# Gathers that convert fp32 rows to fp16 in flight, drains by tile, and a variable lead, in a gather, cumulative sum and matmul kernel

## The chip, the cores and the metric

The kernel runs on one core of one Trainium2 chip. The metric is the time on the device in microseconds (us), as the median over several executions. A ratio between two kernels is the mean time of one kernel's fast runs over the mean of the other's fast runs of the same rounds, so it is not quite the ratio of the medians quoted beside it.

The chips that these runs fell on are of two kinds. On two of them (numbers 1 and 6), and in the recorded result, the kernel before takes 351 us. On five others (2, 7, 10, 13 and 15) the same kernel takes longer. I call these **quick chips** and **slow chips**. Whether it is the chip itself or its condition at the time isn't shown: numbers 10 and 13 were slow in both of their calls, and every other chip was seen in one call only. Within one call the runs of the kernel before lie within 0.7% of each other on a quick chip and within 1 to 3.5% on a slow one. Every call runs the kernel before on the same chip as its experiments.

## The reference

```python
B, S, N, D = (16, 4096, 2048, 512)            # x: fp32 [B, S, D], indices: int64 [B, N], sorted, w: fp32 [D, D]

def reference(x, indices, w):
    gathered = x[np.arange(B)[:, None], indices, :]
    cs = np.cumsum(gathered, axis=1)
    return np.matmul(cs, w).astype(np.float32)
```

The kernel gathers 16 x 2048 rows of 2 KB, 67.1 MB, and writes as many bytes of output. A tile is 128 rows; there are T = 256 tiles, and a pair of tiles is a group g (R = 2, G = 128).

## The kernel before

Each tile goes through seven steps on five engines: GpSimd issues the gather, ScalarE casts the rows to fp16, TensorE sums them with a triangular matrix ("sums"; the result is transposed and lies in PSUM, the memory for TensorE's results), VectorE adds the running total and writes fp16 ("carry"), TensorE multiplies by w ("project"; the result is a "product"), ScalarE copies the product out of PSUM ("drain"), and SyncE starts the store. `Lane.need(sem, value)` waits on a semaphore unless that engine has already waited for as much.

```python
    def gather(t):                                   # GpSimd
        g, r = divmod(t, R)
        if g >= NG // R:                             # NG = 16 tiles of fp32
            pool.need(s_c0, R)
            pool.need(s_c, g - NG // R)              # its buffer is free when its cast is done
        ...
        nc.gpsimd.indirect_dma_start(out=g32[g % (NG // R)][:, r, :], in_=x_flat, ...).then_inc(s_g[t % NG], 16)

    def cast(g):                                     # ScalarE, a pair at a time
        for t in range(R * g, R * g + R):
            act.need(s_g[t % NG], 16 * (t // NG + 1))
        act.need(s_a, R * (g - NH + 1))
        nc.scalar.copy(out=g16[g % NH][:], in_=g32[g % (NG // R)][:]).then_inc(s_c, 1)

    def sums(t, first=0):                            # TensorE: 4 matmuls of 128 columns, after s_c
    def carry(t):                                    # VectorE: adds the last column of the tile before
    def project(g, j, first=0):                      # TensorE: 4 matmuls of 512 columns
    def drain(g):                                    # ScalarE: a pair out of PSUM
    ...
    for g in range(G - 1):                           # the order on ScalarE
        if g + AH + 1 < G - 1:                       # AH = 2
            cast(g + AH + 1)
        ...
        drain(g)
```

ScalarE executes in order, so drain(g) stands behind cast(g + 3).

Of the kernel before, what the change touches and what calls it, by code (L numbers as in the profile page):

```python
# [27 lines left out]
def kernel(  # L28
# [21 lines left out]
    NH = 4  # L50
    NA = 4
    NB = 2
    NC = 4
    NO = 8
    LOOP = 4
    AH = 2
# [13 lines left out]
    ut = const.tile([P, R, Q], FP16)  # L70
    ident = const.tile([P, P], FP32)
    zeros = const.tile([P, D], FP16)
    spare = const.tile([P, 1], FP16)
    g32 = [const.tile([P, R, D], FP32, name=f"g32_{i}") for i in range(NG // R)]
    g16 = [const.tile([P, R, D], FP16, name=f"g16_{i}") for i in range(NH)]
# [3 lines left out]
    pb = [ps.tile([P, R, D], FP32, name=f"pb{i}") for i in range(NB)]  # L79
# [3 lines left out]
    def sem(name):  # L83
        return tc.alloc_semaphore(name)

    s_z, s_ut, s_wc, s_if, s_pt, s_prep, s_c0, s_c1 = (
        sem(f"s_{n}") for n in ("z", "ut", "wc", "if", "pt", "prep", "c0", "c1")
# [8 lines left out]
    s_c = sem("s_c")  # L96
# [9 lines left out]
    def gather(t):  # L106
        g, r = divmod(t, R)
        if g >= NG // R:
            pool.need(s_c0, R)
            pool.need(s_c, g - NG // R)  # L110
# [3 lines left out]
        else:  # L114
# [3 lines left out]
            out=g32[g % (NG // R)][:, r, :],  # L118
# [6 lines left out]
    def cast(g):  # L125
        for t in range(R * g, R * g + R):
            act.need(s_g[t % NG], 16 * (t // NG + 1))
        act.need(s_a, R * (g - NH + 1))
        nc.scalar.copy(out=g16[g % NH][:], in_=g32[g % (NG // R)][:]).then_inc(s_c, 1)  # L129

    def cast_tile(t, done):
        g, r = divmod(t, R)
        act.need(s_g[t % NG], 16 * (t // NG + 1))
        act.need(s_a, R * (g - NH + 1))
        nc.scalar.copy(out=g16[g % NH][:, r], in_=g32[g % (NG // R)][:, r]).then_inc(done, 1)  # L135

    def sums(t, first=0):
        g, r = divmod(t, R)
        if isinstance(first, int):
            if g in (0, G - 1):  # L140
                pe.need(s_c1 if g else s_c0, r + 1)
            else:
                pe.need(s_c, g)
            pe.need(s_ut, 4)
            pe.need(s_d, t - NA + 1)
        elif r == 0:
            nc.tensor.wait_ge(s_c, first + g)
        for c in range(DC):
            mm = nc.tensor.matmul(  # L149
                out=pa[t % NA][:, c],  # L150
                lhsT=g16[g % NH][:, r, c * P : (c + 1) * P],
                rhs=ut[:],
                start=(c == 0),
                stop=(c == DC - 1),
            )
        mm.then_inc(s_a, 1)

    def carry(t):
        g, r = divmod(t, R)
        dve.need(s_b, R * (g - NC + 1))  # L160
        dve.need(s_a, t + 1)
        dst = cst[g % NC][:, :, :, r * Q : (r + 1) * Q]
        if t % NT == 0:
            nc.vector.tensor_copy(out=dst, in_=pa[t % NA][:]).then_inc(s_d, 1)  # L164
            return
        e = (r - 1) % R
        last = cst[(t - 1) // R % NC][:, :, R - 1, e * Q + Q - 1 : e * Q + Q]
        dve.need(s_d, t)
        nc.vector.tensor_tensor(  # L169
            out=dst,  # L170
            in0=pa[t % NA][:],
            in1=last.unsqueeze(2).broadcast_to([P, DC, R, Q]),
            op=mybir.AluOpType.add,
        ).then_inc(s_d, 1)

    def project(g, j, first=0):
        if isinstance(first, int):
            pe.need(s_wc, DC)
            pe.need(s_d, R * (g + 1))
            pe.need(s_e, g - NB + 1)  # L180
        elif j == 0:
            nc.tensor.wait_ge(s_d, R * first + R * (g + 1))
            nc.tensor.wait_ge(s_e, first + (g - NB + 1))
        for c in range(DC):
            mm = nc.tensor.matmul(  # L185
                out=pb[g % NB][:, j],
                lhsT=cst[g % NC][:, c, j, :],
                rhs=w16[:, c, :],
                start=(c == 0),
                stop=(c == DC - 1),  # L190
            )
        mm.then_inc(s_b, 1)

    def drain(g):
        act.need(s_o[g % NO], 16 * (g // NO))
        act.need(s_b, R * (g + 1))
        nc.scalar.copy(out=ob[g % NO][:], in_=pb[g % NB][:]).then_inc(s_e, 1)  # L197

    def store(g):
        b, h = divmod(g, GB)  # L200
        dst = out[b, h * R * P : (h + 1) * R * P, :].rearrange("(p j) d -> p j d", j=R)
        sp.need(s_e, g + 1)
        nc.sync.dma_start(out=dst, in_=ob[g % NO][:]).then_inc(s_o[g % NO], 16)

    def drain_last(j, lane, copy):
        g = G - 1
        lane.need(s_o[g % NO], 16 * (g // NO))
        lane.need(s_b, R * g + j + 1)
        copy(out=ob[g % NO][:, j], in_=pb[g % NB][:, j]).then_inc(s_el[j], 1)  # L209

    def store_last():
        b, h = divmod(G - 1, GB)
        dst = out[b, h * R * P : (h + 1) * R * P, :].rearrange("(p j) d -> p j d", j=R)
        for j in range(R):
            sp.need(s_el[j], 1)
            nc.sync.dma_start(out=dst[:, j], in_=ob[(G - 1) % NO][:, j]).then_inc(s_ol[j], 16)
# [11 lines left out]
    idx_rows = indices.bitcast(U32).rearrange("b (t q) -> (b t) q", q=2 * P)  # L228
    for k in range(KI):
# [3 lines left out]
    for c in range(DC):  # L233
# [144 lines left out]
```

## Time and profile before

| | |
|---|---|
| time, median (recorded result, 4 runs) | 351.19 us (350.31 to 352.29) |
| span of its trace | 451.1 us |
| work that the time must hold | 67.1 MB gathered, 67.1 MB stored, w and the indices: 135.66 MB |

The trace lies 100 us above the timed runs (the prediction had three of these, median 351.63 us). The lines of its trace are shown and read in the prediction below.

### The profile page before, as it was taken

Reading aid. Unit: us, or ns where it says so; the run is one execution under the profiler, and the core shown is the slowest. Engines: PE = TensorE matmul, PEld = TensorE weight load, DVE = VectorE, ACT = ScalarE, POOL = GpSimd, SP = SyncE. Lnnn points to the kernel's source line nnn. Section 1 sums busy time; section 2 is a strip of 40 time slices with the busy share of each in tenths; the row PEclk is TensorE's granted clock in tenths of the full one; section 3 lists DMA queues with packets and bytes.
Section 4 is the critical chain, followed back from the end, with each engine's and each line's share of the span. In section 5 each row is a group of like instructions: output and inputs, shape, how many; then the busy total and the mean of one; then the engine's idle time right before and its main releaser. Section 6 shows DMA issues by size and latency. Waiting matters only on the chain.

```text
span 451.1 us, 6060 instructions
## 1 busy us (share of the span) xinstructions
PE 323.7 (72%) x2069; PEld 170.2 (38%) x2069; DVE 179.5 (40%) x264; ACT 249.4 (55%) x262; POOL 243.8 (54%) x264
## 2 busy tenths in 40 slices
PE   6236678767696966977679766777758776768795
PEld 2113344334343533443344333343334343334352
DVE  3103334434334444444324533444432443333662
ACT  3403546645556656656446745665554664545883
POOL 6773565555565755655565556655556555556300
PEclk9865997969979899889998999898999898899999
DMA  7774998888999999988998999888898888898875
GB/s 225 233 232 141 329 324 274 309 304 306 333 304 345 315 352 336 327 301 307 332 310 280 345 339 331 293 309 300 296 347 313 288 295 306 308 320 314 285 289 232
DMA packets 40476, 135.66 MB, mean 301 GB/s; under 512 B 6800, under 2 KB 7056, under 8 KB 40464
## 3 DMA queue, kind: packets, MB, share of 16 engines
q0 software_dynamic: 20480, 67.13, 48.2%
q1 hardware_dynamic: 19712, 68.43, 37.7%
q14 instruction: 11, 0.09, 0.1%
q10 hardware_dynamic: 272, 0.00, 0.0%
q8 instruction: 1, 0.02, 0.0%
HBM read 68.42 MB, written 67.11 MB: 300 GB/s over the span
## 4 chain that ended last, share of the span: by engine, by line
PE 64%; another core or an unknown queue 14%; DVE 8%; issue 6%; ACT 5%; DMA 2%; DVEq 1%; ACTq 0%; SPq 0%
PE pb L185 51%; PE pa L149 13%; DVE cst L169 8%; ACT ob L197 3%; ACT g L129 2%; DVEq L23 1%; DMA g<-in_x_dram,idx_first 1%; DVE cst L164 0%; DMA idx_first<-in_indices_dram 0%; ACT g L135 0%; ACT ob L209 0%; ACTq L23 0%; SPq L373 0%; SPq L81 0%
## 5 line engine op out<-in xcount | busy, mean ns | idle before, releaser
L185 PE MATMUL pb<-w,cst 128*128 128x512 f16 x1024 | 288.4, 408 | 118.5 <-DVE cst L169 75.8
L117 POOL DMA_INDIRECT g<-in_x_dram,idxg x252 | 238.7, 947 | 178.4 <-ACT g L129 103.9
L169 DVE TENSOR_TENSOR cst<-pa,cst 128x512 f16<-128x512 f32 x240 | 166.0, 692 | 237.9 <-PE pa L149 135.5
L197 ACT COPY ob<-pb 128x1024 f32<-128x1024 f32 x127 | 128.8, 1014 | 186.1 <-PE pb L185 140.5
L185 PEld LDWEIGHTS pb<-w,cst 128*128 128x128 f16 x1024 | 93.4, 104 | 199.4 <-DVE cst L169 57.0
L129 ACT CAST g<-g 128x1024 f16<-128x1024 f32 x126 | 132.4, 1051 | 4.1 <-DMA g<-in_x_dram,idxg 2.8
L149 PEld LDWEIGHTS pa<-ut,g 128*128 128x128 f16 x1024 | 82.5, 102 | 71.0 <-issue 15.7
L149 PE MATMUL pa<-ut,g 128*128 128x128 f16 x1024 | 104.3, 227 | 2.4 <-ACT g L135 1.4
L164 DVE CAST cst<-pa 128x512 f16<-128x512 f32 x16 | 11.0, 686 | 20.1 <-PE pb L185 10.3
L273 PE MATMUL pb<-zeros 128*128 128x512 f16 x19 | 6.4, 503 | 1.5 <-DVE zeros L277 1.5
L117 POOL DMA_INDIRECT g<-in_x_dram,idx_first x4 | 4.0, 996 | 2.3 <-DMA idx_first<-in_indices_dram 1.4
L273 PEld LDWEIGHTS pb<-zeros 128*128 128x128 f16 x19 | 2.3, 125 | 4.4 <-issue 1.9
L135 ACT CAST g<-g 128x512 f16<-128x512 f32 x4 | 2.4, 619 | 1.9 <-DMA g<-in_x_dram,idx_first 1.6
L335 ACT CAST w<-w 128x512 f16<-128x512 f32 x2 | 1.2, 618 | 3.0 <-DMA w<-in_w_dram 3.0
L332 ACT ACT_TABLE_LOAD x1 | 1.3, 1283 | 1.5 <-SPq L81 1.5
L294 DVE CAST w<-w 128x512 f16<-128x512 f32 x2 | 1.1, 552 | 2.4 <-DMA w<-in_w_dram 2.4
L280 DVE CAST idxf<-idx 128x128 f32<-128x128 uint32 x2 | 0.6, 288 | 2.8 <-DMA idx<-in_indices_dram 2.8
L209 DVE COPY ob<-pb 128x512 f32<-128x512 f32 x1 | 0.7, 692 | 1.2 <-PE pb L185 1.2
L209 ACT COPY ob<-pb 128x512 f32<-128x512 f32 x1 | 0.6, 586 | 0.8 <-PE pb L185 0.8
L291 DVE CAST idxg<-pb 128x128 uint32<-128x128 f32 x2 | 0.5, 290 | 0.9 <-PE pb L285 0.9
L277 DVE MEMSET zeros<- 128x256 uint32 x1 | 0.3, 272 | 1.1 <-SPq L81 1.1
L285 PEld LDWEIGHTS pb<-ident,idxf 128*128 128x128 f32 x2 | 0.5, 231 | 0.5 <-issue 0.5
(10 smaller groups left out, 2.2 us busy)
## 6 DMA issues: line engine op xcount, KB each, us to landing
out_dram<-ob SPq DMA_DIRECT2D x127, 512.0 KB
g<-in_x_dram,idxg POOLq DMA_INDIRECT x252
w<-in_w_dram SPq DMA_DIRECT2D x4, 256.0 KB
out_dram<-ob SPq DMA_DIRECT2D x2, 256.0 KB, 2.7
idx<-in_indices_dram SPq DMA_DIRECT2D x2, 128.0 KB, 2.7
g<-in_x_dram,idx_first POOLq DMA_INDIRECT x4
idx_first<-in_indices_dram ACTq DMA_DIRECT2D x1, 2.0 KB, 1.9
idx_first<-in_indices_dram SPq DMA_DIRECT2D x1, 2.0 KB, 2.1
```

The lines of the kernel that those rows point to most:

```text
L23: self.eng.wait_ge(sem, value)
L117: nc.gpsimd.indirect_dma_start(out=g32[g % (NG // R)][:, r, :], out_offset=None, in_=x_flat, in_offset=bass.IndirectOffsetOnAxis(ap=ap, ax ...
L129: nc.scalar.copy(out=g16[g % NH][:], in_=g32[g % (NG // R)][:]).then_inc(s_c, 1)
L135: nc.scalar.copy(out=g16[g % NH][:, r], in_=g32[g % (NG // R)][:, r]).then_inc(done, 1)
L149: mm = nc.tensor.matmul(out=pa[t % NA][:, c], lhsT=g16[g % NH][:, r, c * P : (c + 1) * P], rhs=ut[:], start=(c == 0), stop=(c == DC - 1),)
L164: nc.vector.tensor_copy(out=dst, in_=pa[t % NA][:]).then_inc(s_d, 1)
L169: nc.vector.tensor_tensor(out=dst, in0=pa[t % NA][:], in1=last.unsqueeze(2).broadcast_to([P, DC, R, Q]), op=mybir.AluOpType.add,).then_inc ...
L185: mm = nc.tensor.matmul(out=pb[g % NB][:, j], lhsT=cst[g % NC][:, c, j, :], rhs=w16[:, c, :], start=(c == 0), stop=(c == DC - 1),)
L197: nc.scalar.copy(out=ob[g % NO][:], in_=pb[g % NB][:]).then_inc(s_e, 1)
L209: copy(out=ob[g % NO][:, j], in_=pb[g % NB][:, j]).then_inc(s_el[j], 1)
L273: nc.tensor.matmul(out=pb[NB - 1][:, R - 1], lhsT=zeros[:, :P], rhs=zeros[:], start=True, stop=True)
L332: nc.scalar.copy(out=spare[:], in_=zeros[:, :1])
```

## The change

Its intent is to take the casts off ScalarE, to let a tile's sums start as soon as its rows have landed, and to shorten the start and the end. The gathers write fp16 buffers, so the DMA converts; a gather waits for the sums 16 tiles back. The first and last pair (PLAIN) use a full 128 x 128 triangular matrix, so that their rows come out in order and can be stored by tile. Products and drains go by tile. TensorE's loop is unrolled, in an order in which the sums lead the products by one tile at both ends and by up to four between (the "lead"). The weight loads move ahead of the index loads and are split over two queues.

```diff
-    g32 = [const.tile([P, R, D], FP32, ...) for i in range(NG // R)]
-    g16 = [const.tile([P, R, D], FP16, ...) for i in range(NH)]
+    g16 = [const.tile([P, R, D], FP16, ...) for i in range(NG // R)]
-    pb = [ps.tile([P, R, D], FP32, ...) for i in range(NB)]          # NB = 2
+    pb = [ps.tile([P, D], FP32, ...) for i in range(NB)]             # NB = 4
     def gather(t):
-        if g >= NG // R:
-            pool.need(s_c0, R)
-            pool.need(s_c, g - NG // R)
+        pool.need(s_a, R * (g + 1) - NG)
-            out=g32[g % (NG // R)][:, r, :],
+            out=g16[g % (NG // R)][:, r, :],
-    def cast(g): ...
-    def cast_tile(t, done): ...
     def sums(t, u):
+        pe.need(s_g[t % NG], 16 * (t // NG + 1))
+                rhs=uq[:] if g in PLAIN else ut[:],
+    for c in range(DC):                                   # w, now ahead of the indices
+        eng = (nc.sync, nc.scalar)[c % 2]
+        eng.dma_start(out=w32[:, c, :], ...)
     for k in range(KI):
         nc.sync.dma_start(out=idx64[:, k, :], ...)
-    for c in range(DC):
-        nc.sync.dma_start(out=w32[:, c, :], ...)
-    busy(10)
+    busy(12)                                              # warm-up matmuls on zeros, result unused
+    for u in range(T):
+        lead = min(LEAD, 1 + u // 8, 1 + (T - 1 - u) // 6)    # LEAD = 4
+        first = u if u // R in PLAIN else u // R * R + R - 1
+        while done < T and done <= max(first, u + lead):
+            order.append((True, done))
+            done += 1
+        order.append((False, u))
... (carry, project, drain and store by tile; rows in order for PLAIN; no loop on TensorE)
```

More of the change, by code (lines that the diff above doesn't have):

```diff
@@ L49 @@
     NG = 16
-    NH = 4
+    LEAD = 4
     NA = 4
-    NB = 2
+    NB = 4
     NC = 4
     NO = 8
-    LOOP = 4
-    AH = 2
     assert D == 512 and N % (R * P) == 0 and T % P == 0
@@ L70 @@
     ut = const.tile([P, R, Q], FP16)
+    uq = const.tile([P, P], FP16)
     ident = const.tile([P, P], FP32)
@@ L73 @@
     spare = const.tile([P, 1], FP16)
-    g32 = [const.tile([P, R, D], FP32, name=f"g32_{i}") for i in range(NG // R)]
-    g16 = [const.tile([P, R, D], FP16, name=f"g16_{i}") for i in range(NH)]
+    g16 = [const.tile([P, R, D], FP16, name=f"g16_{i}") for i in range(NG // R)]
     cst = [const.tile([P, DC, R, P], FP16, name=f"cst{i}") for i in range(NC)]
@@ L78 @@
     pa = [ps.tile([P, DC, R, Q], FP32, name=f"pa{i}") for i in range(NA)]
-    pb = [ps.tile([P, R, D], FP32, name=f"pb{i}") for i in range(NB)]
+    pb = [ps.tile([P, D], FP32, name=f"pb{i}") for i in range(NB)]
     ctx.enter_context(tc.tile_critical(no_gpsimd_drain=True))
@@ L84, in sem @@
         return tc.alloc_semaphore(name)
-    s_z, s_ut, s_wc, s_if, s_pt, s_prep, s_c0, s_c1 = (
-        sem(f"s_{n}") for n in ("z", "ut", "wc", "if", "pt", "prep", "c0", "c1")
+    s_z, s_ut, s_wc, s_if, s_pt, s_prep, s_of, s_c = (
+        sem(f"s_{n}") for n in ("z", "ut", "wc", "if", "pt", "prep", "of", "c")
     )
@@ L95 @@
     s_o = [sem(f"s_o{i}") for i in range(NO)]
-    s_c = sem("s_c")
     s_a = sem("s_a")
@@ L123, in gather, with sums @@
         ).then_inc(s_g[t % NG], 16)
-    def cast(g):
-        for t in range(R * g, R * g + R):
-            act.need(s_g[t % NG], 16 * (t // NG + 1))
-        act.need(s_a, R * (g - NH + 1))
-        nc.scalar.copy(out=g16[g % NH][:], in_=g32[g % (NG // R)][:]).then_inc(s_c, 1)
-    def cast_tile(t, done):
-        g, r = divmod(t, R)
-        act.need(s_g[t % NG], 16 * (t // NG + 1))
-        act.need(s_a, R * (g - NH + 1))
-        nc.scalar.copy(out=g16[g % NH][:, r], in_=g32[g % (NG // R)][:, r]).then_inc(done, 1)
-    def sums(t, first=0):
-        g, r = divmod(t, R)
-        if isinstance(first, int):
-            if g in (0, G - 1):
-                pe.need(s_c1 if g else s_c0, r + 1)
-            else:
-                pe.need(s_c, g)
-            pe.need(s_ut, 4)
-            pe.need(s_d, t - NA + 1)
-        elif r == 0:
-            nc.tensor.wait_ge(s_c, first + g)
+    PLAIN = (0, G - 1)
+    def sums(t, u):
+        g, r = divmod(t, R)
+        pe.need(s_g[t % NG], 16 * (t // NG + 1))
+        pe.need(s_d, t - NA + 1)
         for c in range(DC):
+            if c == 1 and u is not None:
+                pe.need(s_e, u - NB + 1)
             mm = nc.tensor.matmul(
                 out=pa[t % NA][:, c],
-                lhsT=g16[g % NH][:, r, c * P : (c + 1) * P],
-                rhs=ut[:],
+                lhsT=g16[g % (NG // R)][:, r, c * P : (c + 1) * P],
+                rhs=uq[:] if g in PLAIN else ut[:],
                 start=(c == 0),
@@ L159, in carry, with project @@
         g, r = divmod(t, R)
-        dve.need(s_b, R * (g - NC + 1))
         dve.need(s_a, t + 1)
-        dst = cst[g % NC][:, :, :, r * Q : (r + 1) * Q]
+        src = pa[t % NA][:]
+        if g in PLAIN:
+            dst = cst[g % NC][:, :, r, :]
+            src = src.rearrange("p c r q -> p c (r q)")
+        else:
+            dst = cst[g % NC][:, :, :, r * Q : (r + 1) * Q]
         if t % NT == 0:
-            nc.vector.tensor_copy(out=dst, in_=pa[t % NA][:]).then_inc(s_d, 1)
+            nc.vector.tensor_copy(out=dst, in_=src).then_inc(s_d, 1)
             return
-        e = (r - 1) % R
-        last = cst[(t - 1) // R % NC][:, :, R - 1, e * Q + Q - 1 : e * Q + Q]
-        dve.need(s_d, t)
-        nc.vector.tensor_tensor(
-            out=dst,
-            in0=pa[t % NA][:],
-            in1=last.unsqueeze(2).broadcast_to([P, DC, R, Q]),
-            op=mybir.AluOpType.add,
-        ).then_inc(s_d, 1)
-    def project(g, j, first=0):
-        if isinstance(first, int):
-            pe.need(s_wc, DC)
-            pe.need(s_d, R * (g + 1))
-            pe.need(s_e, g - NB + 1)
-        elif j == 0:
-            nc.tensor.wait_ge(s_d, R * first + R * (g + 1))
-            nc.tensor.wait_ge(s_e, first + (g - NB + 1))
+        if r == 0:
+            last = cst[(g - 1) % NC][:, :, R - 1, P - 1 : P]
+        elif g in PLAIN:
+            last = cst[g % NC][:, :, r - 1, P - 1 : P]
+        else:
+            last = cst[g % NC][:, :, R - 1, r * Q - 1 : r * Q]
+        dve.need(s_d, t)
+        if g in PLAIN:
+            last = last.broadcast_to([P, DC, P])
+        else:
+            last = last.unsqueeze(2).broadcast_to([P, DC, R, Q])
+        nc.vector.tensor_tensor(out=dst, in0=src, in1=last, op=mybir.AluOpType.add).then_inc(
+            s_d, 1
+        )
+    def project(u, t):
+        g, j = divmod(u, R)
+        pe.need(s_e, u - NB + 1)
+        pe.need(s_d, u + 1 if g in PLAIN else R * (g + 1))
         for c in range(DC):
+            if c == 2 and t is not None:
+                pe.need(s_d, t - NA + 1)
             mm = nc.tensor.matmul(
-                out=pb[g % NB][:, j],
+                out=pb[u % NB][:],
                 lhsT=cst[g % NC][:, c, j, :],
@@ L192, in project, with drain @@
         mm.then_inc(s_b, 1)
-    def drain(g):
-        act.need(s_o[g % NO], 16 * (g // NO))
-        act.need(s_b, R * (g + 1))
-        nc.scalar.copy(out=ob[g % NO][:], in_=pb[g % NB][:]).then_inc(s_e, 1)
+    def drain(u):
+        g, j = divmod(u, R)
+        act.need(s_b, u + 1)
+        nc.scalar.copy(out=ob[g % NO][:, j], in_=pb[u % NB][:]).then_inc(s_e, 1)
     def store(g):
         b, h = divmod(g, GB)
-        dst = out[b, h * R * P : (h + 1) * R * P, :].rearrange("(p j) d -> p j d", j=R)
-        sp.need(s_e, g + 1)
-        nc.sync.dma_start(out=dst, in_=ob[g % NO][:]).then_inc(s_o[g % NO], 16)
-    def drain_last(j, lane, copy):
-        g = G - 1
-        lane.need(s_o[g % NO], 16 * (g // NO))
-        lane.need(s_b, R * g + j + 1)
-        copy(out=ob[g % NO][:, j], in_=pb[g % NB][:, j]).then_inc(s_el[j], 1)
-    def store_last():
-        b, h = divmod(G - 1, GB)
-        dst = out[b, h * R * P : (h + 1) * R * P, :].rearrange("(p j) d -> p j d", j=R)
-        for j in range(R):
-            sp.need(s_el[j], 1)
-            nc.sync.dma_start(out=dst[:, j], in_=ob[(G - 1) % NO][:, j]).then_inc(s_ol[j], 16)
+        rows = out[b, h * R * P : (h + 1) * R * P, :]
+        if g in PLAIN:
+            for j in range(R):
+                sp.need(s_e, R * g + j + 1)
+                done = s_ol[j] if g else (s_o[0], s_of)[j]
+                nc.sync.dma_start(
+                    out=rows[j * P : (j + 1) * P, :], in_=ob[g % NO][:, j]
+                ).then_inc(done, 16)
+            return
+        sp.need(s_e, R * (g + 1))
+        nc.sync.dma_start(
+            out=rows.rearrange("(p j) d -> p j d", j=R), in_=ob[g % NO][:]
+        ).then_inc(s_o[g % NO], 16)
     with nc.allow_non_contiguous_dma(reason="a few indices, one per partition"):
@@ L228 @@
     idx_rows = indices.bitcast(U32).rearrange("b (t q) -> (b t) q", q=2 * P)
+    for c in range(DC):
+        eng = (nc.sync, nc.scalar)[c % 2]
+        eng.dma_start(out=w32[:, c, :], in_=w[c * P : (c + 1) * P, :]).then_inc(s_w[c], 16)
     for k in range(KI):
@@ L232 @@
         ).then_inc(s_idx[k], 16)
-    for c in range(DC):
-        nc.sync.dma_start(out=w32[:, c, :], in_=w[c * P : (c + 1) * P, :]).then_inc(s_w[c], 16)
-    for g in range(G - 1):
+    for g in range(G):
         store(g)
-    store_last()
     for g in range(G - NO, G - 1):
@@ L264 @@
     ).then_inc(s_ut, 1)
+    nc.gpsimd.memset(uq[:], 1.0).then_inc(s_ut, 1)
+    pool.need(s_ut, 5)
+    nc.gpsimd.affine_select(
+        out=uq[:],
+        in_=uq[:],
+        compare_op=mybir.AluOpType.is_ge,
+        fill=0.0,
+        base=0,
+        pattern=[[1, P]],
+        channel_multiplier=-1,
+    ).then_inc(s_ut, 1)
     for t in range(T):
@@ L273, in busy @@
             nc.tensor.matmul(
-                out=pb[NB - 1][:, R - 1], lhsT=zeros[:, :P], rhs=zeros[:], start=True, stop=True
+                out=pb[NB - 1][:], lhsT=zeros[:, :P], rhs=zeros[:], start=True, stop=True
             )
@@ L285 @@
         nc.tensor.transpose(
-            out=pb[k % NB][:, 0, :P], in_=idxf[:, k, :], identity=ident[:]
+            out=pb[k % NB][:, :P], in_=idxf[:, k, :], identity=ident[:]
         ).then_inc(s_pt, 1)
-    busy(10)
+    busy(12)
     for k in range(KI):
         dve.need(s_pt, k + 1)
-        nc.vector.tensor_copy(out=idxg[:, k, :], in_=pb[k % NB][:, 0, :P]).then_inc(s_prep, 1)
+        nc.vector.tensor_copy(out=idxg[:, k, :], in_=pb[k % NB][:, :P]).then_inc(s_prep, 1)
     for c in range(DC // 2, DC):
@@ L296 @@
         carry(t)
-    drain_last(0, dve, nc.vector.tensor_copy)
-    def step(g, first=0):
-        for j in range(R):
-            project(g, j, first)
-            if not isinstance(first, int) or g + AH < G:
-                sums(R * (g + AH) + j, first)
-    for t in range(R):
-        sums(t)
-    pe.need(s_prep, KI)
-    for j in range(R):
-        project(0, j)
-        sums(R + j)
-    for t in range(2 * R, R * (AH + 1)):
-        sums(t)
-    for g in range(1, LOOP):
-        step(g)
-    with nc.tensor.Fori(LOOP, G - LOOP, LOOP) as first:
-        for g in range(LOOP):
-            step(g, first)
-    for g in range(G - LOOP, G - AH - 1):
-        step(g)
-    project(G - 3, 0)
-    project(G - 3, 1)
-    sums(T - 2)
-    project(G - 2, 0)
-    sums(T - 1)
-    project(G - 2, 1)
-    project(G - 1, 0)
-    project(G - 1, 1)
+    pe.need(s_ut, 6)
+    pe.need(s_prep, KI)
+    order = []
+    done = 0
+    for u in range(T):
[5 more added lines that the diff above has]
+        order.append((False, u))
+    for i, (is_sums, t) in enumerate(order):
+        after = next((v for k, v in order[i + 1 :] if k != is_sums), None)
+        if is_sums:
+            sums(t, after)
+        else:
+            pe.need(s_wc, DC)
+            project(t, after)
     act.need(s_z, 1)
@@ L335 @@
         nc.scalar.copy(out=w16[:, c, :], in_=w32[:, c, :]).then_inc(s_wc, 1)
-    for t in range(R):
-        cast_tile(t, s_c0)
-    for g in range(1, AH + 1):
-        cast(g)
-    for g in range(G - 1):
-        if g + AH + 1 < G - 1:
-            cast(g + AH + 1)
-        elif g + AH + 1 == G - 1:
-            for t in range(T - R, T):
-                cast_tile(t, s_c1)
-        drain(g)
-    drain_last(1, act, nc.scalar.copy)
+    for u in range(T):
+        if u % R == 0:
+            if u == R * NO:
+                act.need(s_of, 16)
+            act.need(s_o[u // R % NO], 16 * (u // R // NO))
+        drain(u)
 _INS = ['x', 'indices', 'w']
```

## The prediction

> **What bounds the kernel now.** I first set the profiled execution beside the timed ones: the trace spans 451.1 us, the timed runs have a median of 351.63 us. So about 100 us of the trace is not in the timed runs, and I use its durations of single operations and its order of events, not its span. Then I read the DMA part of the page, because 135.66 MB in 351.63 us is 386 GB/s.
>
> ```profile
> DMA packets 40476, 135.66 MB, mean 301 GB/s; under 512 B 6800, under 2 KB 7056, under 8 KB 40464
> q0 software_dynamic: 20480, 67.13, 48.2%
> q1 hardware_dynamic: 19712, 68.43, 37.7%
> ```
>
> Queue q0 carries the gathers, q1 the stores. The last column is the time that the packets took, as a share of 16 engines' span. The stores took 0.377 x 451.1 = 170.1 us for 68.43 MB, which is 402 GB/s; the gathers 0.482 x 451.1 = 217.4 us for nearly the same bytes, 309 GB/s. The two sum to 387.5 us, more than a whole timed run, so the gathers' packets can't be that slow when nothing is recorded. I take 402 GB/s for both, an estimate: 135.66 MB / 402 GB/s = **337.5 us of DMA work**, 96% of the timed median. Next, the stretches:
>
> ```profile
> core 0: us, PE busy (x) PEld busy (x) DVE busy (x) ACT busy (x) POOL busy (x), PEclk, DMA share, GB/s
> 0.00:4.50 4.50, 3.03 (x8) 1.11 (x9) 0.58 (x2) 1.48 (x2) 2.21 (x9) 1.00 0.37 88
> 4.50:18.20 13.70, 7.37 (x47) 3.76 (x45) 3.95 (x9) 6.51 (x8) 10.35 (x12) 1.00 0.85 262
> ...
> 424.00:446.00 22.00, 21.50 (x150) 11.45 (x147) 12.57 (x19) 16.86 (x19) 1.01 (x2) 1.00 0.75 288
> 446.00:451.10 5.10, 0.08 (x1) 0.00 (x0) 0.02 (x1) 0.59 (x1) 0.00 (x0) 0.85 0.53 206
> ```
>
> The last column says what both ends lose against 402 GB/s: 4.5 x (1 - 88/402) = 3.5 us before the first gather, 13.7 x (1 - 262/402) = 4.8 us until the first store, 22.0 x (1 - 288/402) = 6.2 us after the last gather is issued, 5.1 x (1 - 206/402) = 2.5 us at the very end. That is 17 us, and 337.5 + 17 = 354.5 us, 0.8% from the timed median. So my reading is: **the DMA engines bound the middle, and the two ends are what is lost**. Now the engines:
>
> ```profile
> L117 POOL DMA_INDIRECT g<-in_x_dram,idxg x252 | 238.7, 947 | 178.4 <-ACT g L129 103.9
> L197 ACT COPY ob<-pb 128x1024 f32<-128x1024 f32 x127 | 128.8, 1014 | 186.1 <-PE pb L185 140.5
> L129 ACT CAST g<-g 128x1024 f16<-128x1024 f32 x126 | 132.4, 1051 | 4.1 <-DMA g<-in_x_dram,idxg 2.8
> L209 ACT COPY ob<-pb 128x512 f32<-128x512 f32 x1 | 0.6, 586 | 0.8 <-PE pb L185 0.8
> ```
>
> Where GpSimd waits for nothing, its gathers start 0.947 + 0.30 = 1.25 us apart (at 20 to 36 us, for instance), so 256 of them need 256 x 1.25 = 320 us: the second bound, close behind. TensorE in the undisturbed tail takes a pair of tiles every 2.17 us (project at 432.59, 434.76, 436.94 us in the timeline), so 128 x 2.17 = 278 us. ScalarE has 132.4 + 128.8 + 3 = 264 us, VectorE 240 x 0.692 + 16 x 0.686 = 177 us. None of these three is at the bound. GpSimd's 103.9 us behind the ScalarE cast is a buffer wait: ScalarE executes in order, and a cast queued behind a drain that waits for TensorE or for a store frees its fp32 buffer late. Back pressure from full queues would look like this, so the big number doesn't promise 100 us.
>
> **What the Trainium skill says.** "DMA: Bandwidth & Descriptors", section "SWDGE vs HWDGE vs iDMA": a DMA that casts has to be issued from GpSimd. These gathers already are, so the change moves no transfer to another queue. No page I found gives the rate of a casting transfer; that is the main unknown. The same page, section "Where 436 GB/s comes from", puts the ceiling of the 16 engines at 435 GB/s; the 402 GB/s of the stores sits under it, which agrees. "Perfetto Trace Analysis", GPSIMD part of "Per-engine timelines", advises timing GpSimd by the start-to-start spacing, not by the reported duration; so I use 1.25 us, not 0.947. "TensorE: Matmul & The Clock Gate", section "Wait — 56ns, not 53.3ns?", has 215.7 and 55.6 ns per matmul at 512 and 128 columns: four of each are 1085 ns per tile, and the trace's 2.17 us per pair agrees.
>
> **The change, part by part.** (1) *Gathers convert.* 126 casts of 1.051 us and 4 small ones go: 135 us of ScalarE work. The bytes read from HBM stay 67 MB; the bytes written to SBUF halve. If an engine's time goes by the bytes it reads, as 4 KB packets read from HBM and stored to HBM suggest by sharing one size, the 337.5 us stay. I choose that. The chain from landing to sums loses a cast (0.6 us for a tile, 1.05 us for a pair) and the wait for its pair. (2) *Drains by tile.* 256 copies of 0.586 us, 150 us, in place of 129 us. ScalarE falls from 264 to about 152 us, off any path. The product buffers are four of one tile in place of two of two: the same space. (3) *Buffers.* The gathered rows had 16 fp32 tiles and, behind them, 8 fp16 tiles; now there are 16 fp16 tiles, and a gather waits for the sums 16 tiles back, no longer for the cast. That couples GpSimd to TensorE directly: with sums at most 4 tiles ahead of products, TensorE needs 1.09 us per tile against GpSimd's 1.25, so I expect it to keep up. (4) *Start.* In the kernel before, the first drain stands behind the cast of pair 3, so the first store waits for the eighth gather: 18.2 us. Now tile 0 needs two gathers: the first lands near 8.3 us (issued at 3.38, 4.94 us in the chain of waits), then sums 0.4, carry 0.7, product 1.0, drain 0.6 and some handoffs of 0.1 to 0.2 us: the store at about 12 us. Six us earlier is 6 / 1.25, about 5 tiles of 262 KB, 1.3 MB moved in time that was half idle: **3.3 us saved**. Against it, the indices come behind two weight loads on their queue, about 1 us later; the fifth gather, at 8.6 us, had some 2.4 us of slack (indices converted by 6.2 us), so it costs 0 to 1 us. The second triangular matrix on GpSimd (two operations of some 0.2 to 0.3 us) lies before the first gather's wait. (5) *End.* The old order leaves products of two to three pairs after the last sums; the new one lets the lead fall to one tile and stores the last pair by tile in row order. Of the 8.7 us that the tail loses I give it **2.5 us**. (6) *Middle.* The loop on TensorE is unrolled, so more instructions are fetched, 2048 matmuls with their weight loads; beside 135 MB that is nothing. A drain blocked on a store no longer holds a cast. Whether the timed runs lose anything there I can't see; the sum above leaves no room (354.5 against 351.63), the trace shows a DMA share of 0.89. I give it **3 us**. Sum: 351.6 - 3.3 - 2.5 - 3 = 342.8, with 0 to 1 us back for the indices and a similar gain if the pair-wise waits shrink. I say **342 us**.
>
> **The rivals.** *GpSimd becomes the bound.* If halving the bytes written makes the gathers cheaper, the DMA work falls below 320 us and the issue pace rules: 3.4 + 320 us, then about 10 us to land, compute and store the last tiles: 333 us. For it: 320 is only 5% under 337. Against it: the read side stays the same. *The converting packets are slower*, or the descriptors take GpSimd longer. Gathers are half of the 337.5 us, so each 10% on their packets adds 17 us and gives 359 us; twice as slow would give over 500 us. Likewise each 10% on 1.25 us adds 32 us to GpSimd's 320, and at 1.38 us it would be the bound at about 365 us. Nothing in this trace speaks about it, since no gather in it converts; the weight of the finely tuned rest of the change speaks against a disaster. *Hidden anyway*: the 135 us of ScalarE were never on the path, the ends move by 2 to 3 us, and the time is 346 to 351 us. For it: the bound is the same data through the same engines. *A new wait*: fewer buffered tiles make TensorE's pauses reach GpSimd; 345 to 355 us.
>
> **Range and chances.** The main line at 342 us lies 2.7% below the median; the 2% border is 344.6 us, so small errors in the ends cross it. GpSimd as the bound sets the low end, 332 us; mildly slower packets or a new wait set the high end, 354 us. Weights: main line 45%, GpSimd bound 17%, hidden or new wait 25%, dearer gathers 13%. With most of the first two and a little of the third below the border: faster 0.57, within 2% 0.30, slower 0.13.
>
> **What the changed kernel's profile would show.** Right: q0 with half the megabytes at about the same share of time or less; the cast line gone; first store near 12 us; gathers still 1.25 us apart when free; ScalarE near 152 us busy; fewer us between the last gather's issue and the end than 27. Wrong: a q0 share above 48.2% (dearer packets), gathers spaced above 1.25 us without a wait (dearer descriptors), GpSimd waiting on the sums line for longer than the 103.9 us it waited for casts, or TensorE gaps in the middle with the DMA share falling below 0.89. The prediction fails upward if conversion costs an engine time per row, downward if an engine's time goes by bytes written.

## The result, and the profile after

| | median us | runs | range us |
|---|---|---|---|
| before | 351.19 | 4 | 350.31 to 352.29 |
| after | 356.65 | 4 | 356.07 to 357.17 |

The ratio is 1.0153, with a 95% interval of 1.0118 to 1.0189: slower by 1.5%, clear of noise though inside the 2% that counts as the same, and outside the range that I gave. A second call on a quick chip gave 357.23 us against 351.37 us, ratio 1.0150.

The DMA part of the changed kernel's page answers to the queue lines of the prediction. The columns are packets, MB, and the time of the packets as a share of 16 engines' span.

```profile
span 354.4 us, 5499 instructions
DMA packets 57018, 102.35 MB, mean 289 GB/s; under 512 B 6816, under 2 KB 39840, under 8 KB 56992
q0 software_dynamic: 36864, 33.57, 58.1%
q1 hardware_dynamic: 19568, 67.91, 50.8%
```

The gathers' megabytes are halved, since the profile counts what is written. But their packets went from 20480 to 36864. In both kernels 4096 of them are the completion signals (256 gathers on 16 engines). The other 16384 had carried two rows of 2 KB each; now 32768 packets carry one row each. The share of q0 rose from 48.2% to 58.1%, but of different spans: in time it is 217 us (0.482 x 451.1) on a slow chip before and 206 us (0.581 x 354.4) now. So these two traces alone don't show dearer packets; a_plain4 below gives the fair comparison. The two shares sum to 109%: packets overlap in time, so a share is not a plain utilisation.

The engines, from the groups of the page (line, engine, operation, count; busy us and mean ns; idle time before and what ended most of it):

```profile
L112 POOL DMA_INDIRECT g<-in_x_dram,idxg x252 | 236.7, 939 | 82.1 <-issue 57.8
L185 ACT COPY ob<-pb 128x512 f32<-128x512 f32 x256 | 150.1, 586 | 194.7 <-PE pb L173 194.7
L130 PEld LDWEIGHTS pa<-ut,g 128*128 128x128 f16 x1008 | 65.7, 98 | 124.1 <-DMA g<-in_x_dram,idxg 101.1
```

ScalarE lost its casts, as planned, and no gain from it shows in the total. GpSimd takes 0.939 + 0.30 us per gather, as before, so descriptors for a converting gather are not dearer. The third line shows the new wait: TensorE's weight loads for the sums idle 101.1 us until a gather lands. The chain that ended last (followed back from the last instruction, at each step to what released it) says the same:

```profile
DMA 62%; POOL 15%; PE 14%; issue 6%; DVE 1%; SPq 0%; ACT 0%
DMA g<-in_x_dram,idxg 61%; POOL g L112 15%; PE pb L173 8%; PE pa L130 4%; DMA idx<-in_indices_dram 1%; PE pb L269 1%; DVE cst L162 1%; SPq L216 0%; DVE cst L149 0%; PE pb L281 0%; ACT ob L185 0%; SPq L207 0%; DVE idxf L276 0%; SPq L351 0%; SPq L79 0%
```

The middle, as a stretch from 60 to 320 us (busy us of each engine, then the granted clock, the DMA share and GB/s):

```profile
60.00:320.00 260.00, 232.98 (x1579) 111.55 (x1579) 136.25 (x197) 115.47 (x197) 192.43 (x206) 1.00 1.13 300
```

A tile now moves 128 rows of 1 KB in and 2 KB out, 393,216 bytes as counted. At 300 GB/s that is **1.311 us per tile**, and 256 tiles make 335.5 us; the remaining 18.9 us of the span are the ends. This tile time is the number that the experiments turn on.

### The profile page after: what moved, and what is told of

It reads as the page before. It is cut to its first block, busy times and chain, and to the rows that moved or that the text cites. A ratio compares the mean times of both kernels' runs of the same rounds, so it can differ in the third digit from the quotient of the medians.

```text
span 354.4 us, 5499 instructions
## 1 busy us (share of the span) xinstructions
PE 310.2 (88%) x2071; PEld 148.7 (42%) x2071; DVE 179.0 (51%) x263; ACT 152.7 (43%) x260; POOL 242.1 (68%) x266
## 3 DMA queue, kind: packets, MB, share of 16 engines
q0 software_dynamic: 36864, 33.57, 58.1%
## 4 chain that ended last, share of the span: by engine, by line
DMA 62%; POOL 15%; PE 14%; issue 6%; DVE 1%; SPq 0%; ACT 0%
DMA g<-in_x_dram,idxg 61%; POOL g L112 15%; PE pb L173 8%; PE pa L130 4%; DMA idx<-in_indices_dram 1%; PE pb L269 1%; DVE cst L162 1%; SPq L216 0%; DVE cst L149 0%; PE pb L281 0%; ACT ob L185 0%; SPq L207 0%; DVE idxf L276 0%; SPq L351 0%; SPq L79 0%
## 5 line engine op out<-in xcount | busy, mean ns | idle before, releaser
L173 PE MATMUL pb<-w,cst 128*128 128x512 f16 x1024 | 262.5, 379 | 4.4 <-DVE cst L162 3.7
L185 ACT COPY ob<-pb 128x512 f32<-128x512 f32 x256 | 150.1, 586 | 194.7 <-PE pb L173 194.7
L130 PE MATMUL pa<-ut,g 128*128 128x128 f16 x1008 | 98.5, 220 | 31.5 <-DMA g<-in_x_dram,idxg 29.1
L130 PEld LDWEIGHTS pa<-ut,g 128*128 128x128 f16 x1008 | 65.7, 98 | 124.1 <-DMA g<-in_x_dram,idxg 101.1
L173 PEld LDWEIGHTS pb<-w,cst 128*128 128x128 f16 x1024 | 89.2, 98 | 67.2 <-DVE cst L162 4.6
L269 PE MATMUL pb<-zeros 128*128 128x512 f16 x21 | 7.9, 549 | 1.5 <-DVE zeros L273 1.5
L130 PEld LDWEIGHTS pa<-uq,g 128*128 128x128 f16 x16 | 1.1, 98 | 0.7
L130 PE MATMUL pa<-uq,g 128*128 128x128 f16 x16 | 1.4, 219 | 0.0
```

Source lines behind the costliest of these rows:

```text
L130: mm = nc.tensor.matmul(out=pa[t % NA][:, c], lhsT=g16[g % (NG // R)][:, r, c * P : (c + 1) * P], rhs=uq[:] if g in PLAIN else ut[:], star ...
L173: mm = nc.tensor.matmul(out=pb[u % NB][:], lhsT=cst[g % NC][:, c, j, :], rhs=w16[:, c, :], start=(c == 0), stop=(c == DC - 1),)
L185: nc.scalar.copy(out=ob[g % NO][:, j], in_=pb[u % NB][:]).then_inc(s_e, 1)
L269: nc.tensor.matmul(out=pb[NB - 1][:], lhsT=zeros[:, :P], rhs=zeros[:], start=True, stop=True)
```

## The experiments

My theory 1: a converting gather sends one row per packet and so costs DMA time in a kernel that is bound by DMA. Rival A: the start, the order or the unrolled loop lose the time, and the conversion doesn't matter. Rival B: GpSimd now waits for sums 16 tiles back (24.0 us in the table of waits), and TensorE's pauses reach it.

### 1. First call: conversion alone, conversion undone, more buffers

It ran four kernels: the kernel before for a profile (b_again), and three experiments.

b_conv, the kernel before with converting gathers. Three things have to go with the conversion: the casts become one-column copies that only pass the signal on, a gather waits for the sums 16 tiles back as in the changed kernel, and the loop body holds eight pairs in place of four:

```diff
-        if g >= NG // R:
-            pool.need(s_c0, R)
-            pool.need(s_c, g - NG // R)
+        pool.need(s_a, R * (g + 1) - NG)
-            out=g32[g % (NG // R)][:, r, :],
+            out=g16[g % (NG // R)][:, r, :],
-        nc.scalar.copy(out=g16[g % NH][:], in_=g32[g % (NG // R)][:]).then_inc(s_c, 1)
+        nc.scalar.copy(out=spare[:, g + 8 : g + 9], in_=zeros[:, :1]).then_inc(s_c, 1)
-    LOOP = 4
+    LOOP = 8          # the sums in the loop now index 8 pair buffers
... (cast_tile in the same way; buffers; the sums read the 8 pair buffers)
```

a_plain, the changed kernel with plain gathers and ScalarE casts (a pair in the middle, a tile in the first and last pair), at most two tiles ahead of what TensorE's order needs:

```diff
+    g32 = [const.tile([P, R, D], FP32, ...) for i in range(NG // R)]
-        pool.need(s_a, R * (g + 1) - NG)
+        if g >= NG // R:
+            pool.need(s_c, cast_no(R * (g - NG // R) + 1))
-        pe.need(s_g[t % NG], 16 * (t // NG + 1))
+        pe.need(s_c, cast_no(t))
     for u in range(T):                       # ScalarE
+        ahead = min(2, u // 4, (T - 1 - u) // 4)
+        while ready < T and ready <= max(first, u + lead) + ahead:
+            cast(ready)
+            ready += 1
         drain(u)
... (cast, cast_no; the sums read 4 pair buffers of fp16)
```

a_deep: `NG = 16` becomes `NG = 32`.

> The kernel before, unchanged, for a profile that isn't stretched to 451 us. If plain gathers put two rows of 2 KB into a packet and the converting ones one row, the plain packets take about 159 ns again and the span is about 350 us, with about 1.29 us of DMA work per tile. If the gathers of the kernel before were really as slow as its first trace said (mean 210 ns per 4 KB packet), the mean stays near 210 ns.

> The kernel before with converting gathers alone: its ScalarE casts become one-column copies that only pass the signal on, and a gather waits for the sums 16 tiles back. Theory 1 (one row per packet costs DMA time): slower than before by 6 to 9 us, 357 to 361 us, and the packets of its gathers number 36864 as in the changed kernel. Rival A (the lost gain lies in the new start, the order or the unrolled loop): within 2 us of before, 349 to 353 us.

> The changed kernel with plain fp32 gathers again and casts on ScalarE, by pair in the middle and by tile in the first and last pair; its start, end and lead stay. Theory 1: the conversion cost 6 to 9 us and the ends won 2 to 4 us, so 346 to 350 us, faster than both. Rival A: 355 to 358 us, as the changed kernel.

> The changed kernel with 32 instead of 16 buffers for gathered tiles. Rival B (GpSimd now waits for the sums 16 tiles back, and TensorE's pauses reach it; 24 us of such waits in the profile): the waits go and the time falls by 3 us or more, to 353 us or less. Theory 1: the DMA engines are full anyway, so the time stays within 1.5 us of 356.65 us.

The call fell on a slow chip. The kernel before took 456.93 us there (11 runs), b_again 461.2 us in its one run, b_conv 405.88 us, a_plain 444.37 us, a_deep 421.5 us. None of the expected times applies, as they were made for 351 us; b_conv's gathers did make the 36864 packets that were expected. Two things follow. The first trace's 451 us belong to such a chip and not to the recording. And on such a chip b_conv's edit gains 11% (ratio of b_conv 0.8896, interval 0.8846 to 0.8945), the opposite sign. Rival B can't be judged by a_deep in the state of the recorded result; on slow chips its 32 buffers gained nothing over the changed kernel (421.5 us, against 409.57 us in its one run on another slow chip).

### 2. In search of a quick chip

> The changed kernel with plain fp32 gathers and ScalarE casts, once more: the first four runs fell on a chip on which the kernel before takes 457 us. If this chip gives 351 us for the kernel before: Theory 1 (one row per packet costs DMA time) 346 to 350 us; Rival A (start, order or unrolled loop) 355 to 358 us. If it gives 457 us again: about 444 us, as then.

> The changed kernel itself. On a chip that gives 351 us for the kernel before: 356 to 357 us again. On one that gives 457 us, where the conversion alone gave 405.9 us and the changed kernel with 32 buffers 421.5 us: if the conversion is what helps there, 405 to 425 us.

> The changed kernel with plain gathers and ScalarE casts, in search of a chip that gives 351 us for the kernel before. There Theory 1 (the conversion puts one row into a packet and so costs DMA time, the ends win a little) expects 346 to 350 us, with 159 ns per packet of 4 KB and 16384 of them; Rival A (start, order or unrolled loop lose it) 355 to 358 us. On a chip that gives 457 us: 444 us again, which decides nothing.

> The kernel before with converting gathers alone, again in search of a chip that gives 351 us for the kernel before. There Theory 1 (one row per packet costs DMA time) expects 357 to 361 us, slower than before by 6 to 9 us; Rival A (start, order or unrolled loop lose the time) 349 to 353 us. On a chip that gives 457 us: 406 us again, which decides nothing.

> The kernel before with converting gathers alone, on whatever chip comes. On one that gives 351 us for the kernel before: Theory 1 (one row per packet costs DMA time) 357 to 361 us; Rival A (start, order or unrolled loop lose the time) 349 to 353 us. On one that gives 457 us: 405 us, which decides nothing.

a_plain2 and a_plain3 gave 445.21 and 450.45 us, b_conv2 and b_conv3 405.19 and 409.53 us, all on slow chips (before: 455 to 461 us); they repeat the first call and decide nothing more. after_again fell on a quick chip and repeated the result: 357.23 us against 351.37 us.

### 3. The index loads ahead of the weight loads

a_idx is the changed kernel with the two groups of loads swapped back, and with it went the kernel before once more for a profile.

> The changed kernel with the index loads ahead of the weight loads, as in the kernel before (its fp32 conversion of the indices began at 4.19 us there and at 7.03 us in the changed kernel, and its first sums at 12.1 us though the first rows had landed long before). Theory 1 with a late start as a second cause: the first store comes 1.5 to 3 us earlier and the time falls by 0.5 to 2 us, to about 355 us on a chip that gives 351 us for the kernel before. If the start is hidden: no change, 356 to 357 us.

> The kernel before, for a profile in the state of the timed runs. Theory 1: 16384 gather packets of 4 KB at about 159 ns in place of the mean of 210 ns, and a span of about 350 us. If this chip is one that gives 457 us, the profile says nothing new.

Again a slow chip: a_idx 405.96 us, b_again2 453.49 us, before 456.48 us. The time says nothing about a quick chip, but the start can be read in the two traces, since it comes ahead of the full queues. The timeline of the changed kernel (start us, duration us, engine, line, operation):

```profile
7.03 0.56 DVE L276 CAST idxf<-idx 128x128 f32<-128x128 uint32 x2 [5.62 <-DMA idx<-in_indices_dram]
7.87 4.38 PE L269 MATMUL pb<-zeros 128*128 128x512 f16 x12
12.08 0.61 PE L130 MATMUL pa<-uq,g 128*128 128x128 f16 x8
15.02 1.43 SPq L194 DMA_DIRECT2D out_dram<-ob  x2
```

and of a_idx:

```profile
4.41 0.23 DVE L276 CAST idxf<-idx 128x128 f32<-128x128 uint32 x1 [2.99 <-DMA idx<-in_indices_dram]
5.84 2.75 PE L269 MATMUL pb<-zeros 128*128 128x512 f16 x12
8.43 0.83 PE L130 MATMUL pa<-uq,g 128*128 128x128 f16 x8
11.36 4.10 SPq L194 DMA_DIRECT2D out_dram<-ob  x2
```

Behind the weight loads the conversion of the indices starts 2.6 us later. The transposes of the indices and twelve warm-up matmuls stand on TensorE ahead of the first sums, so these start at 12.08 in place of 8.43 us, and the first store at 15.02 in place of 11.36 us. Not all of these 3.7 us come from the order of the loads: the warm-up matmuls took 4.38 us in one trace and 2.75 us in the other. In after_third, a later trace of the changed kernel, they take 2.75 us too:

```profile
7.72 2.75 PE L269 MATMUL pb<-zeros 128*128 128x512 f16 x12
10.31 0.61 PE L130 MATMUL pa<-uq,g 128*128 128x128 f16 x8
13.24 1.43 SPq L194 DMA_DIRECT2D out_dram<-ob  x2
```

Against this one the order of the loads costs the first store 1.9 us; what that is worth in the end wasn't measured on a quick chip.

### 4. The deciding call: conversion undone and conversion alone, on a quick chip

> The changed kernel, first on this chip, to show which state the chip is in and to stand beside the two below: 356 to 357 us in the state of the recorded result, 405 to 425 us in the other.

> The changed kernel with plain gathers and ScalarE casts. In the state of the recorded result (351 us before): Theory 1 (one row per packet costs DMA time) 346 to 350 us with 16384 gather packets of about 159 ns; Rival A (start, order, unrolled loop) 355 to 358 us. In the other state 445 us.

> The kernel before with converting gathers alone. In the state of the recorded result: Theory 1 357 to 361 us; Rival A 349 to 353 us. In the other state 406 us.

This call fell on a quick chip.

| kernel | median us | ratio to before (95%) | us per tile, 60 to 320 us | rest of the span, us |
|---|---|---|---|---|
| before | 351.64 | 1 | no trace | |
| b_conv4: before + conversion | 357.12 | 1.0145 (1.0106 to 1.0183) | 1.311 | 20.5 |
| after_third: the changed kernel | 356.19 (one run) | | 1.311 | 18.9 |
| a_plain4: the changed kernel without conversion | 355.84 | 1.0114 (1.0075 to 1.0153) | 1.266 | 29.9 |

The fourth column is the bytes of a tile over the GB/s of that stretch, the last the span less 256 of them. For a_plain4 a tile is 524,288 bytes:

```profile
60.00:320.00 260.00, 235.19 (x1618) 116.31 (x1616) 139.75 (x203) 203.63 (x304) 196.62 (x209) 1.00 1.03 414
```

and for b_conv4 393,216 bytes:

```profile
60.00:320.00 260.00, 226.04 (x1578) 115.00 (x1576) 136.29 (x198) 109.95 (x198) 191.36 (x204) 1.00 1.13 300
```

b_conv4 meets theory 1 at the low edge of 357 to 361 us and refutes rival A as the whole story: **the conversion, in the old order and with a loop, makes the kernel before slower by 5.5 us**. Its gathers make 36864 packets and 58.1% too. The two converting kernels have the same middle, whatever their order. The rest of the change shows no effect on top of the conversion: the ratios are 1.0145 here and 1.0153 and 1.0150 for the changed kernel.

Rival B goes with the conversion in every pair of kernels (the plain ones also have eight more tiles of buffers), so no run on a quick chip separates it, but the traces answer it. The wait and the median time from issue to landing of a gather, in the changed kernel:

```profile
POOL g L112 <- PE pa L130: 24.0, 62, 0.8
g<-in_x_dram,idxg POOLq DMA_INDIRECT x252, 14.7
```

By the packet records, from 60 to 320 us at least 4 gathers are always issued and not yet landed, and at least 16 packets, as many as there are engines, are in progress in over 99% of the time, in b_conv4 as well. So GpSimd's waits left the DMA engines hardly any time without work.

a_plain4 misses its expectation of 346 to 350 us. Its middle went the way that theory 1 said: 1.266 in place of 1.311 us per tile, which over 256 tiles is 11.5 us. Its queues on the page:

```profile
DMA packets 40636, 135.92 MB, mean 384 GB/s; under 512 B 6816, under 2 KB 7072, under 8 KB 40608
q0 software_dynamic: 20480, 67.13, 48.9%
q1 hardware_dynamic: 19568, 67.91, 47.6%
POOL 46%; DMA 18%; issue 17%; PE 13%; ACT 4%; DVE 1%; SPq 0%; ACTq 0%
```

With two rows per packet the gathers' share falls from 58.1% to 48.9% of nearly the same span (206 to 173 us), and the chain that ended last is now GpSimd's: it issues a gather every 1.25 us and waits only 3.4 us for casts. So this middle may be paced by GpSimd and no longer by the DMA; the 11.5 us are then the cost of the conversion against GpSimd's pace, and the DMA work alone may have grown by more. But its ends take 29.9 us in place of 18.9, which gives the 11 us back. The timeline shows where part of it goes; the packet records have the last gathered row landed at 338.2 us:

```profile
341.38 0.59 ACT L205 COPY ob<-pb 128x512 f32<-128x512 f32 x1 [1.52 <-PE pb L193]
341.86 0.62 ACT L141 CAST g<-g 128x512 f16<-128x512 f32 x1
342.53 0.46 PE L150 MATMUL pa<-uq,g 128*128 128x128 f16 x4 [1.25 <-ACT g L141]
342.79 1.91 PE L193 MATMUL pb<-w,cst 128*128 128x512 f16 x4
344.74 0.59 ACT L205 COPY ob<-pb 128x512 f32<-128x512 f32 x1 [2.26 <-PE pb L193]
345.22 0.62 ACT L141 CAST g<-g 128x512 f16<-128x512 f32 x1
```

The cast of the last tile stands behind two drains until 345.22 us, 7 us after its rows were there, and TensorE, idle between, runs its four products in 1.91 us in place of 1.03. That is a fault of where I put the casts, not of plain gathers. So undoing the conversion showed the cost of the conversion in the middle, and hid it in the total.

### 5. The last call: a shorter end, and conversion without fewer bytes

a_best is a_plain with the loads swapped as in a_idx and the casts kept two tiles ahead to the end:

```diff
-        ahead = min(2, u // 4, (T - 1 - u) // 4)
+        ahead = 2 if u > 1 else 0
```

a_best_r changes one thing in a_best, `g32` from FP32 to float32r. The Trainium skill, "DMA: Bandwidth & Descriptors", section "SWDGE vs HWDGE vs iDMA", says that a float32r destination always casts. The bytes written stay the same, so this parts "converts" from "writes half".

> The changed kernel, first in the call, as in the call that fell into the state of the recorded result: 356 to 357 us there.

> The kernel before, for a profile in the state of the timed runs. The conversion explanation needs a middle of 1.25 to 1.27 us per tile (410 GB/s and more), 16384 gather packets of about 159 to 167 ns in place of the 210 ns of its first trace, and more time lost at the ends than in the changed kernel (18.8 us by then). If its middle also takes 1.31 us per tile, the conversion is not the cause.

> Plain gathers with ScalarE casts in the changed kernel, casts now two tiles ahead up to the end (in the run before, the last pair's casts stood 3 us behind drains, and its end took 16 us after the last gather had landed), and the index loads ahead of the weight loads. If the conversion costs 1.31 in place of 1.25 us per tile and the ends can be kept short: 345 to 350 us, faster than both kernels. If the rest of the change costs the time by itself: 354 us or more.

> The kernel of the run before this one with one edit: the gathers' destination is float32r, which converts but writes as many bytes as it reads. If a converting gather is dear because it puts one row into a packet: 32768 gather packets, 1.30 us or more per tile in the middle, and 8 us or more above the run before this one. If what matters is the halved size of what is written (1 KB per row): 16384 packets and the same time as the run before this one, within 2 us.

It fell on a slow chip: before 456.81 us (11 runs), after_fourth 409.57 us and b_again3 459.76 us in one run each, a_best 450.13 us (443 to 455), a_best_r 449.05 us (445 to 451), both unclear against the kernel before. Whether a_best beats the kernel before on a quick chip stays open, and so does the profile of the kernel before there. The count of packets does not depend on the chip. The DMA part for a_best:

```profile
q0 software_dynamic: 20480, 67.13, 49.3%
```

and for a_best_r:

```profile
q0 software_dynamic: 36864, 67.13, 56.1%
```

The same 67.13 MB, written as 4-byte elements, go out in 36864 packets as soon as the gather converts. So **it is the conversion that puts one row into a packet, not the halved row**. In time the two didn't differ: by their fast runs 446.5 us for a_best and 448.4 us for a_best_r, which is within the noise, and the 8 us that I expected were not seen. So doubling the packets did not cost time on a slow chip; on a quick chip the pair wasn't run.

## Why the prediction was wrong

**The bound: right for the changed kernel, not shown for the one before.** In the changed kernel TensorE waits for gathers, GpSimd waits only 24.0 us, and the gathers make 61% of the chain. The estimate of 402 GB/s for full queues was near: a_plain4 moves 414 GB/s in the middle. The reason that I gave for the slow first trace was wrong: the profiled run itself was slow. That my sum came within 0.8% of the timed median was in part luck: the ends in it are read from that slow trace, and the stretch from 18.2 to 40 us, at 214 GB/s, isn't in it. Two smaller readings were off as well: packets' times overlap, so a sum of 387.5 us beyond the timed run doesn't by itself show that the packets were faster there (the changed kernel's shares sum to 109% of its own span); and ScalarE's 264 us count overlaps, the page has 249.4. In a_plain4, with plain gathers on a quick chip, GpSimd paces the middle, so the second bound, "close behind", may have been the first one in the kernel before.

**The step that failed** is part (1): "If an engine's time goes by the bytes it reads [...] the 337.5 us stay. I choose that." I took over the count of packets without looking at what it was made of. The page of the kernel before had it: 20480 packets less 4096 signals are 16384 for 32768 rows. In their place there came 32768 packets of one row. In the packet records on quick chips a plain packet of two rows has a median of 159 ns (a_plain4), a converting one of one row 96 to 98 ns. Those durations overlap their neighbours (the DMA share is 1.13 in one kernel and 1.03 in the other), so the honest measure is the tile: 1.311 against 1.266 us, **11.5 us over 256 tiles that my sum had at zero**. What the splitting alone costs can only be estimated: the stores' packets of 2 KB have a median of 84 ns in a_plain4, so splitting one of 159 ns in two would cost 2 x 84 - 159 = 9 ns, and 4 more packets per engine and tile make 36 of the 45 ns. No run on a quick chip splits packets without converting, so how much of the cost is the count of packets and how much the converting itself stays open; that the conversion as a whole costs it is what b_conv4 and a_plain4 show.

**The start: the mechanism right, a term mis-sized.** I said the first store would come at about 12 us, with 0 to 1 us for the indices behind the weights. It came at 15.02 us (13.24 to 16.10 in three quick traces, with 2.75 to 5.23 us of warm-up matmuls); with the old order of the loads it comes at 11.36 us (on a slow chip). The order costs 1.9 us. I had counted only the slack of the fifth gather and overlooked that the transposes and warm-up matmuls stand on TensorE ahead of the first sums.

**The end: not as said.** The span from the last gather's issue (326.0 us) to the end is 28 us, where I wanted fewer than 27. The last gather takes 20 us from issue to landing, and by the packet records 12 tiles are still on their way when GpSimd is done. After the last row has landed (345.9 us) 8.5 us remain, which is short.

**The gains of both ends and the middle, 8.8 us in my sum.** No quick trace of the kernel before exists. If its middle takes 1.266 us per tile, as a_plain4's does, its ends take about 350 - 324 = 26 us (an estimate, with 350 us for its span), against 20.5 in b_conv4 and 18.9 in the changed kernel. By that estimate the ends won 7 us, 5.4 us of it already in b_conv4, and the sum is -7 + 11.5 = +4.5 us, where +5.5 was measured. The sum is no check, since the ends are by definition the span less the middle. If the estimate holds, the gains of 8.8 us were sized well enough in total, and the gather was not; a quick profile of the kernel before, with a middle of 1.25 to 1.27 us per tile, would show it, and none was had.

**The rivals.** "The converting packets are slower" came true, to 13% of the chances and with too large a figure for 10% (17 us), because packets overlap. GpSimd as the bound is what the kernel becomes without conversion, not with it. The sign that I named for dearer packets, q0 above 48.2%, came out at 58.1%, but by luck: the 48.2% belong to a slow trace, and only because a_plain4 has 48.9% on a quick chip does the comparison hold. ScalarE at 152.7 us was as said, and nothing of it shows in the total.

## What to carry to other kernels

Where DMA is the bound, count packets and not only bytes: before a gather is made to convert, divide its rows by its packets, and ask whether rows that now share a packet will still do so. Work taken off an engine that isn't the bound, as ScalarE's casts here, bought nothing in the middle on the quick chip, and at most something at the ends. And before a trace is used for sizes, check its span against the timed runs and against the time of the profiled run itself; if they differ, look for the reason in the machine as well as in the recording.

## What the Trainium skill lacked or had wrong

- "DMA: Bandwidth & Descriptors", section "SWDGE vs HWDGE vs iDMA", says where casts must be issued but not what they cost. Here a converting gather of 2 KB rows makes 32768 packets in place of 16384, for fp16 and for float32r, and with fp16 a tile takes 1.311 in place of 1.266 us.
- The same section prefers packets of up to 4096 B. Plain gathers keep to that (two rows of 2 KB); converting ones stop at one row.
- The same page, section "Why small descriptors are slow (HBM only)", puts the fixed cost of a packet at about 3 cycles and packetization as worth it only at 256 B or less. Here plain packets of 2 and 4 KB take 84 and 159 ns, by which one more packet costs 9 ns (an estimate), and converting gathers that read 2 KB per packet came with a loss of 1.5%; how much of it is the packets isn't separated.
- "HBM Reference", section "Specifications (TRN2)", gives one bandwidth for a core that streams alone and a lower one for two cores that stream at once. No page has two kinds of chip: the same kernel took 351 us on two chips and 455 to 461 us on five, and the changed kernel 356 and 410 us. Why is open.
